# Two blocks on one core: the low weights' buffers and the low parts of the streamed operands at other places in a partition

## The chip, the cores and the metric

The kernel runs on one core of a Trainium2 chip. The metric is the device time of one execution in microseconds. TensorE multiplies, VectorE (DVE) and ScalarE (ACT) do elementwise work, GpSimd (POOL) helps, and SyncE (SP) issues most of the transfers. The operands lie in the core's on-chip memory, which has 128 partitions; an address below is a byte offset within a partition, and it is the same in all 128.

## The reference

Two blocks run one behind the other on 256 tokens of width 1024, all in float32. The first is one layer, the second adds 16 meta tokens (272 in all) and has two layers:

```python
# first block (first_block, hybrid_layer)
h = rmsnorm(x); proj = h @ w_in            # q, k, v, z, beta, decay, LRU input and gate
mix = concat(gated delta rule, gated linear recurrence)
x = x + mix @ w_out
u = relu(rmsnorm(x) @ w_ff1); x = x + (u * u) @ w_ff2      # d_ff 4096
# second block, twice
h = h + 0.5 * swiglu(rmsnorm(h))                           # d_ff 2816
h = h + mixer(rmsnorm(h))    # stick-breaking attention, a 31-tap convolution, two gates, w_out
h = h + 0.5 * swiglu(rmsnorm(h))
```

Each block ends in an RMS norm, and the meta tokens are dropped at the end. The second layer of the second block needs the meta tokens only for its first swiglu and for keys, values and the convolution, so part of its work runs on 256 tokens.

## The kernel before

**Products in two parts.** Nearly all time goes into products of a weight matrix with an activation of 256 or 272 columns. Both are split into a high part (rounded to float32r) and a low part (the rest). `job` (L508) makes one 128-row tile of a product: for each slice k of 128 rows it issues three matmuls into one PSUM bank, high weights times high activation (L534), high weights times low activation (L535) and low weights times high activation (L536). The weights are the stationary operand, 128 x 128, loaded anew for each matmul; the activation is streamed, 128 x 256 or 128 x 272.

**The weights.** `emit_dma` (L449) brings chunks of the packed weights into `raw` buffers. `emit_high` (L467) copies a unit of up to eight slices into one of five `wh` buffers on ScalarE. `emit_split` (L483) subtracts on VectorE (for some units on GpSimd) and writes one of four `wl` buffers. All `wh` and `wl` buffers are 4096 bytes, and slice s of a unit starts 512 s bytes into its buffer. The pools are opened in the order const, raw, wh, wl, small, tmp, and then the pool of each phase, and they lie in memory in that order.

**The streamed operands.** A class `XS` (L641) holds an activation as a high and a low tile, `hi(k)` and `lo(k)`. The narrow ones (8 slices) use one of two places in the const pool, `x0` and `x1`, each a pair of tiles (`x00`, `x01` and `x10`, `x11`) with a step of 320 elements (1280 bytes) at 272 columns and 256 elements at 256. Before each pair lies an unused tile `skew0` or `skew1` of `SKEW[i]` elements (L672). The wide ones, `hid` (32 slices in the first block, 22 in the swiglus), are two tiles of a pool of their own; the high one starts `pad` elements into its tile, with `pad` from `HSKEW`. Its keys are "ff1" for the first block and (first or second swiglu, layer) for the second. 

**Which stage reads what.** In the order of time: the projections of the first block read x0 (24 tiles), its w_out x1 (8), ff1 x0 (32) and ff2 `hid` "ff1" (8 tiles of 32 slices), all with 256 columns. Then, with 272 columns: layer 0's first gate/up (44 tiles) reads x1 and its down (8 tiles of 22 slices) `hid` (0,0); its mixer reads x0 (36 tiles), the attention's and the convolution's outputs in x1 and w_out's operand `mo` in x0; its second gate/up reads x1 and its down `hid` (1,0); layer 1's first gate/up reads x0, its down `hid` (0,1). Layer 1's mixer reads x1, partly with 272 columns and, for q and the gates, with 256 columns from token 16 on, which starts each slice 64 bytes later. Then 256 columns to the end: the attention's and convolution's outputs in x0, `mo` in x1, the last gate/up in x0 and the last down in `hid` (1,1).

**Order.** The order of the instructions on each engine is fixed when the program is written. A planner keeps an estimated clock for each engine (`clk`, advanced by `op` and by `job`) and interleaves the elementwise flows with the matmuls by it. Its costs depend on the engine, the kind of operation and the number of columns.

Of the kernel before, what the change touches and what calls it, by code (L numbers as in the profile page):

```python
# [7 lines left out]
F32 = mybir.dt.float32  # L8
F32R = mybir.dt.float32r
# [9 lines left out]
KD = 8  # L19
# [3 lines left out]
MIX1 = 17100  # L23
MIX2 = 16200
XW = 320
SKEW = (32, 32)
HSKEW = {"ff1": 56, (0, 0): 24, (0, 1): 8, (1, 0): 40, (1, 1): 40}
LEAD = 3
MINLEAD = 2
RAW = 3  # L30
# [195 lines left out]
def tile_hybrid_blocks(  # L226
# [13 lines left out]
    const = ctx.enter_context(tc.tile_pool(name="const", bufs=1))  # L240
    rawp = ctx.enter_context(tc.tile_pool(name="raw", bufs=RAW))
    whp = ctx.enter_context(tc.tile_pool(name="wh", bufs=LEAD + 2))
    wlp = ctx.enter_context(tc.tile_pool(name="wl", bufs=LEAD + 1))
    small = ctx.enter_context(tc.tile_pool(name="small", bufs=2))
    tmp = ctx.enter_context(tc.tile_pool(name="tmp", bufs=1))
# [90 lines left out]
    def start_flow(gen, rank=0, limit=None):  # L336

        f = Flow(gen)
        f.limit = limit
        f.t, f.eng, f.rank = main.t, "P", rank  # L340
        flows.append(f)
        flows.sort(key=lambda f: f.rank)
        return f
# [95 lines left out]
    def cv(name, i=None):  # L439
        o, w = CST[name]  # L440
        return C[:, o:o + w] if i is None else C[:, o + i:o + i + 1]
# [66 lines left out]
    def job(kind, x, n, o=0, bank_=None, last=True, start=None):  # L508


        j = job_no[0]
        job_no[0] += 1
        assert jobs[j][0] == kind, (jobs[j], kind)
        first = bank_ is None if start is None else start
        if bank_ is None:
            if len(free_banks) < 3:
                force(lambda: len(free_banks) >= 3)
            bank_ = free_banks.pop(0)
        acc = bank_[:, 0:n]
        mine = job_units[j]  # L520
        total = sum(len(units[u][1]) for u in mine)
        done = 0
        for u in mine:
            st["unit"] = u
            emit_split(u + MINLEAD)
            h, lo = wh.pop(u), wl.pop(u)
            clk["P"] = max(clk["P"], w_at.pop(u) + LAT)
            for i, k in enumerate(units[u][1]):
                if x.ev[k].t is None:
                    force(lambda: x.ev[k].t is not None)  # L530
                clk["P"] = max(clk["P"], x.ev[k].t + LAT)
                s = slice(128 * i, 128 * i + 128)
                xh, xl = x.hi(k, o, n), x.lo(k, o, n)
                nc.tensor.matmul(acc, h[:, s], xh, start=first and done == 0, stop=False)  # L534
                nc.tensor.matmul(acc, h[:, s], xl, start=False, stop=False)  # L535
                nc.tensor.matmul(acc, lo[:, s], xh, start=False, stop=last and done == total - 1)  # L536
                done += 1
                clk["P"] += 3 * n / 2400 + 0.007
                main.t, main.eng = clk["P"], "P"
                tick()  # L540
        return bank_
# [99 lines left out]
    class XS:  # L641

        def __init__(self, n, k=KD, pool=None, name=None, place=None, first=0, pad=0):
            w = -(-n // 64) * 64
            if pool is not None:
                self.place = None
                both = []
                for i in range(2):  # L650
                    t = pool.tile([128, k * w + pad * (i == 0)], F32R, name=f"{name}{i}")
                    both.append(t[:, pad * (i == 0):])
            else:
                self.place = place or places.pop(0)
                both = [p[:, first * w:(first + k) * w] for p in self.place]
            self.h, self.l = [a.rearrange("p (a b) -> p a b", a=k)[:, :, 0:n] for a in both]
            self.n = n
            self.ev = [Event() for _ in range(k)]
# [10 lines left out]

    places = []  # L670
    for i in range(2):
        const.tile([128, SKEW[i]], F32, name=f"skew{i}")  # L672
        places.append(tuple(const.tile([128, KD * XW], F32R, name=f"x{i}{j}") for j in range(2)))

    def X(k):
        return H[:, k, NM:T2]
# [50 lines left out]
    def first_norm():  # L727
        for k in range(KD):
            cur[0].t = 5.5 if k < 4 else 7.7
            now(split_scaled(X(k), cv("norm_mix_w", k), xa.hi(k), xa.lo(k)))  # L730
            note(xa.ev[k])
            if k < KD - 1:
                yield "W"
# [4 lines left out]
    f = start_flow(first_norm())  # L738
# [521 lines left out]
    for i, (c, t) in enumerate(ORDER1):  # L1260
        off = {"q": 0, "k": 4, "v": 8}.get(c, 0)
        b = job(c.upper(), xa, T1)
# [46 lines left out]
    for m in range(0, KD, 2):  # L1309
        if len(free_banks) < 3:  # L1310
            force(lambda: len(free_banks) >= 3)
        b = free_banks.pop(0)
# [4 lines left out]
    for m in range(0, KD, 2):  # L1317
        b = held[m // 2]
# [9 lines left out]
    phase = ExitStack()  # L1328
    hid = XS(T1, FF1, phase.enter_context(tc.tile_pool(name="ff1", bufs=1)), "hid", pad=HSKEW["ff1"])

# [84 lines left out]
    def swiglu(x, ev_r, o, n, next_g, old_phase, skew, final=False):  # L1415

        old_phase.close()
        phase = ExitStack()
        hid = XS(n, FF2, phase.enter_context(tc.tile_pool(name="ff2", bufs=1)), "hid", pad=HSKEW[skew])
        first = T2 - x.n  # L1420

        def half(ev):
            yield from wait(ev_r)
            ts(R5[:, 0:n], R[:, 0:n], 0.5, MUL)
            note(ev)

        def evac(ga, ua, m):
            yield from wait(ev_r)
            gs, hs_ = (yield from slot()), (yield from slot())
            g, h = gs[:, 0:n], hs_[:, 0:n]  # L1430
            tt(g, ga[:, 0:n], R[:, 0:n], MUL)
            give(ga)
            act(g, g, AF.Silu)
            yield "V"
            tt(h, g, ua[:, 0:n], MUL)
            give(ua)
            free_tmps.append(gs)
            yield from split(h, hid.hi(m), hid.lo(m))
            free_tmps.append(hs_)
            note(hid.ev[m])  # L1440

        ev5 = Event()
        start_flow(half(ev5))
        for m in range(FF2):
            if m == 0 and "gate" in PAIRED:
                ga, ua = pair(("gate", "up"), x, n, o - first)
            else:
                ga = job("gate", x, n, o - first)
                ua = job("up", x, n, o - first)
            start_flow(evac(ga, ua, m))  # L1450
        x.done()
        nx = None if final else XS(T2)
        ev_sq = Event()
        force(lambda: ev5.t is not None and (final or ev_h.t is not None))
        for m in range(KD):
            b = job("down", hid, n)
            if final and m == KD // 2:
                act(warm, ones[:, 0:1], AF.Sqrt)
            start_flow(
                residual(b, m, nx, None if final else next_g(m), acc1[:, 0:n], ev_sq, o, R5[:, 0:n])  # L1460
            )
        return nx, ev_sq, phase
# [281 lines left out]
    def norm_of(n, ev_sq):  # L1744
        ev = Event()
        start_flow(norm_rows(acc1[:, 0:n], n, 1.0 / 1024, 1e-6, R[:, 0:n], [ev_sq], ev, RC[:, 0:len(starts(n))]))
        return ev

    x, ph, ev_r = xc, ff1_phase, ev_r3
    for layer in range(2):  # L1750
        o = NM * layer
        n = T2 - o
        x, ev_sq, ph = swiglu(x, ev_r, 0, T2, lambda m: cv(f"mix_norm_2.{layer}", m), ph, (0, layer))
        x, ev_sq, ph = mixer(x, norm_of(T2, ev_sq), layer, lambda m: cv(f"ffn2_norm_2.{layer}", m), ph)
        x, ev_sq, ph = swiglu(x, norm_of(n, ev_sq), o, n, lambda m: cv("ffn1_norm_2.1", m), ph, (1, layer), final=layer == 1)
# [112 lines left out]
```

## Time and profile before

| | |
|---|---|
| runs | 1538.99, 1542.58, 1542.88 us, median 1542.58 |
| the profiled execution | 1540.48 us, its span 1538.8 |
| mean granted TensorE clock | 0.993 |
| TensorE, VectorE, ScalarE, GpSimd busy | 97%, 70%, 52%, 13% of the span |
| transfers | 248.58 MB, mean 162 GB/s |

The numbers behind the table come from one execution. A row of a timeline has the start in us, the duration, engine, line, operation, the tiles written and read, and the shapes. Matmuls overlap: the time from one start to the next is what one of them costs in a row of many.

### The profile page before, as it was taken

Reading aid. Unit: us, or ns where it says so; the run is one execution under the profiler, and the core shown is the slowest. Engines: PE = TensorE matmul, PEld = TensorE weight load, DVE = VectorE, ACT = ScalarE, POOL = GpSimd, SP = SyncE. Lnnn points to the kernel's source line nnn. Section 1 sums busy time; section 2 is a strip of 40 time slices with the busy share of each in tenths; the row PEclk is TensorE's granted clock in tenths of the full one; section 3 lists DMA queues with packets and bytes.
Section 4 is the critical chain, followed back from the end, with each engine's and each line's share of the span. In section 5 each row is a group of like instructions: output and inputs, shape, how many; then the busy total and the mean of one; then the engine's idle time right before and its main releaser. Section 6 shows DMA issues by size and latency. Waiting matters only on the chain.

```text
span 1538.8 us, 29451 instructions
## 1 busy us (share of the span) xinstructions
PE 1500.2 (97%) x12120; PEld 1480.3 (96%) x12120; DVE 1076.6 (70%) x1882; ACT 803.3 (52%) x1365; POOL 199.6 (13%) x236
## 2 busy tenths in 40 slices
PE   7999999999999999999999999999999999999997
PEld 6989999999999999998999999999999989999997
DVE  5887866667665668998766655655568996866654
ACT  4568666544544445555544444444444655654542
POOL 3230300000000022234400000000003234500000
PEclk9999999999999999999999999999999999999999
DMA  6312455554554444433555444545454433555552
GB/s 225 137 56 83 165 192 192 190 187 144 193 189 159 174 164 164 138 111 110 181 180 187 164 170 160 192 175 178 162 175 161 165 110 127 176 204 182 184 179 76
DMA packets 36376, 248.58 MB, mean 162 GB/s; under 512 B 3984, under 2 KB 5264, under 8 KB 12304
## 3 DMA queue, kind: packets, MB, share of 16 engines
q1 hardware_dynamic: 35248, 245.50, 45.5%
q8 instruction: 95, 1.56, 0.4%
q10 hardware_dynamic: 992, 1.19, 0.2%
q14 instruction: 41, 0.34, 0.1%
HBM read 245.63 MB, written 1.05 MB: 160 GB/s over the span
## 4 chain that ended last, share of the span: by engine, by line
PE 85%; DVE 10%; ACT 3%; issue 1%; POOL 1%; DMA 0%; DVEq 0%; SPq 0%; ACTq 0%; POOLq 0%
PE bank L535 27%; PE bank L536 27%; PE bank L534 27%; PE bank L319 4%; DVE arena L288 2%; DVE arena L299 2%; DVE wl L288 2%; DVE bank L299 1%; ACT arena L276 1%; PE bank L323 1%; DVE x L288 1%; DVE arena L315 1%; ACT wh L276 1%; POOL acc L311 0%; ACT x L276 0%
## 5 line engine op out<-in xcount | busy, mean ns | idle before, releaser
L534 PE MATMUL bank<-x,wh 128*128 128x272 f32 (+1 forms) x2752 | 797.9, 290 | 9.8 <-ACT x L276 9.2
L536 PE MATMUL bank<-x,wl 128*128 128x272 f32 (+1 forms) x2752 | 786.9, 286 | 5.5 <-DVE wl L288 4.7
L535 PE MATMUL bank<-x,wh 128*128 128x272 f32 (+1 forms) x2752 | 787.3, 286 | 2.9 <-DVE x L288 2.2
L288 DVE TENSOR_TENSOR wl<-raw,wh 128x1024 fp32r<-128x1024 f32 (+4 forms) x453 | 532.9, 1178 | 199.0 <-PE bank L536 175.6
L276 ACT ACTIVATE wh<-raw 128x1024 fp32r<-128x1024 f32 (+4 forms) x510 | 494.6, 976 | 271.2 <-PE bank L535 162.4
L534 PEld LDWEIGHTS bank<-x,wh 128*128 128x128 f32 x2752 | 521.5, 190 | 12.9 <-ACT x L276 10.1
L536 PEld LDWEIGHTS bank<-x,wl 128*128 128x128 f32 x2752 | 521.6, 190 | 6.6 <-DVE wl L288 5.7
L535 PEld LDWEIGHTS bank<-x,wh 128*128 128x128 f32 x2752 | 522.0, 190 | 6.2 <-DVE x L288 4.4
L535 PE MATMUL bank<-hid,wh 128*128 128x272 f32 (+1 forms) x960 | 274.5, 286 | 0.0
L536 PE MATMUL bank<-hid,wl 128*128 128x272 f32 (+1 forms) x960 | 274.5, 286 | 0.0
L534 PE MATMUL bank<-hid,wh 128*128 128x272 f32 (+1 forms) x960 | 274.5, 286 | 0.0
L536 PEld LDWEIGHTS bank<-hid,wl 128*128 128x128 f32 x960 | 181.7, 189 | 0.0
L535 PEld LDWEIGHTS bank<-hid,wh 128*128 128x128 f32 x960 | 180.6, 188 | 0.0
L534 PEld LDWEIGHTS bank<-hid,wh 128*128 128x128 f32 x960 | 180.6, 188 | 0.0
L493 POOL TENSOR_TENSOR wl<-raw,wh 128x512 fp32r<-128x512 f32 (+3 forms) x57 | 107.2, 1891 | 190.7 <-ACT wh L276 93.0
L288 DVE TENSOR_TENSOR tmp<-bank,R 128x272 f32<-128x272 f32 (+1 forms) x184 | 78.9, 430 | 68.1 <-PE bank L536 67.3
L276 ACT ACTIVATE tmp<-tmp 128x272 f32<-128x272 f32 (+1 forms) x140 | 59.3, 425 | 115.0 <-DVE tmp L288 78.7
L299 DVE SCALAR_TENSOR_TENSOR bank<-arena,C,bank 128x272 f32<-128x272 f32 (+1 forms) x232 | 102.4, 492 | 3.7 <-ACT bank L276 2.5
L1481 POOL MEMSET arena<- 64x1088 f32 (+1 forms) x4 | 3.9, 976 | 773.9 <-PE bank L536 773.9
L288 DVE TENSOR_TENSOR hid<-tmp,hid 128x272 fp32r<-128x272 f32 (+1 forms) x120 | 51.8, 433 | 38.0 <-ACT hid L276 38.0
L276 ACT ACTIVATE x<-H,C 128x272 fp32r<-128x272 f32 (+2 forms) x64 | 30.0, 486 | 83.5 <-DVE H L288 83.1
L276 ACT ACTIVATE hid<-tmp 128x272 fp32r<-128x272 f32 (+1 forms) x120 | 51.0, 426 | 42.3 <-DVE tmp L288 40.6
(200 smaller groups left out, 948.6 us busy)
## 6 DMA issues: line engine op xcount, KB each, us to landing
raw<-in_w_dram SPq DMA_DIRECT2D x187, 1024.0 KB, 4.8
raw<-in_w_dram SPq DMA_DIRECT2D x32, 960.0 KB, 4.7
raw<-in_w_dram SPq DMA_DIRECT2D x16, 896.0 KB, 4.6
raw<-in_w_dram SPq DMA_DIRECT2D x2, 512.0 KB, 5.9
H<-in_xt_dram SPq DMA_DIRECT2D x1, 544.0 KB, 6.5
LG<-in_lgw_dram SPq DMA_DIRECT2D x1, 512.0 KB, 6.0
out_dram<-H SPq DMA_DIRECT2D x2, 256.0 KB, 2.2
LM<-in_cm_dram SPq DMA_DIRECT2D x1, 320.0 KB, 5.2
```

The source lines that it names most:

```text
L276: nc.scalar.activation(out, in_, func, scale=scale, **kw)
L288: nc.vector.tensor_tensor(out=out, in0=a, in1=b, op=fn)
L299: nc.vector.scalar_tensor_tensor(out=out, in0=a, scalar=s, in1=b, op0=op0, op1=op1)
L315: nc.vector.tensor_tensor_scan(out=out, data0=a, data1=b, initial=initial, op0=op0, op1=op1)
L319: nc.tensor.matmul(out, lhsT, rhs, start=start, stop=stop)
L323: nc.tensor.transpose(out, in_, identity)
L493: nc.gpsimd.tensor_tensor(out=lo[:, 0:n], in0=raw[c][:, o:o + n], in1=wh[i][:, 0:n].bitcast(F32), op=SUB)
L534: nc.tensor.matmul(acc, h[:, s], xh, start=first and done == 0, stop=False)
L535: nc.tensor.matmul(acc, h[:, s], xl, start=False, stop=False)
L536: nc.tensor.matmul(acc, lo[:, s], xh, start=False, stop=last and done == total - 1)
L1481: nc.gpsimd.memset(QZ[i].f[64 * (1 - i):64 * (1 - i) + 64], 0.0)
```

## The change

The tile `gap` of 64 bytes stands in a pool between `wh` and `wl`, and nothing reads or writes it. The unused tiles `skew0` and `skew1` go; in their stead each tile of x0 and x1 has a lead of its own, and `hid`'s low tile has one too.

```diff
-SKEW = (32, 32)
-HSKEW = {"ff1": 56, (0, 0): 24, (0, 1): 8, (1, 0): 40, (1, 1): 40}
+SKEW = ((64, 16), (48, 0))
+HSKEW = {"ff1": (40, 16), (0, 0): (40, 32), (1, 0): (40, 48), (0, 1): (40, 16), (1, 1): (40, 0)}
...
     whp = ctx.enter_context(tc.tile_pool(name="wh", bufs=LEAD + 2))
+    skew = ctx.enter_context(tc.tile_pool(name="skew", bufs=1))
+    skew.tile([128, 16], F32, name="gap")
     wlp = ctx.enter_context(tc.tile_pool(name="wl", bufs=LEAD + 1))
...
-        def __init__(self, n, k=KD, pool=None, name=None, place=None, first=0, pad=0):
+        def __init__(self, n, k=KD, pool=None, name=None, place=None, first=0, pad=(0, 0)):
...
                 for i in range(2):
-                    t = pool.tile([128, k * w + pad * (i == 0)], F32R, name=f"{name}{i}")
-                    both.append(t[:, pad * (i == 0):])
+                    t = pool.tile([128, k * w + pad[i]], F32R, name=f"{name}{i}")
+                    both.append(t[:, pad[i]:])
...
     for i in range(2):
-        const.tile([128, SKEW[i]], F32, name=f"skew{i}")
-        places.append(tuple(const.tile([128, KD * XW], F32R, name=f"x{i}{j}") for j in range(2)))
+        both = [const.tile([128, SKEW[i][j] + KD * XW], F32R, name=f"x{i}{j}") for j in range(2)]
+        places.append(tuple(b[:, a:] for a, b in zip(SKEW[i], both)))
```

What this does to the addresses follows from the declared sizes, tile by tile in their order and each rounded up to 32 bytes. x0's pair starts at 36,096 and 46,336 before, at 36,224 and 46,528 after; x1's at 56,704 and 66,944, then 56,960 and 67,200; the first `wh` buffer at 104,640, then 104,896; the first `wl` buffer at 125,120, then 125,440; the phases' pools at 152,992, then 153,312. The table gives the start of each streamed operand, and of `wl`, less the start of `wh`, modulo 256 bytes. Slices (steps of 512, 1024 or 1280 bytes) and buffers (4096) do not change these numbers.

| operand | before: hi, lo | after: hi, lo | after: lo less `wl` |
|---|---|---|---|
| `wl` | 0 | 64 | |
| x0 | 64, 64 | 192, 0 | 192 |
| x1 | 192, 192 | 192, 192 | 128 |
| x1 read from token 16 on | 0, 0 | 0, 0 | 192 |
| `hid` "ff1" | 192, 192 | 192, 0 | 192 |
| `hid` (0,0) | 64, 64 | 192, 64 | 0 |
| `hid` (1,0) | 128, 128 | 192, 128 | 64 |
| `hid` (0,1) | 0, 0 | 192, 0 | 192 |
| `hid` (1,1) | 128, 128 | 192, 192 | 128 |

## The prediction

> **What bounds the kernel now.** First the page: the busy line and the chain that ended last.
>
> ```profile
> span 1538.8 us, 29451 instructions
> ...
> PE 1500.2 (97%) x12120; PEld 1480.3 (96%) x12120; DVE 1076.6 (70%) x1882; ACT 803.3 (52%) x1365; POOL 199.6 (13%) x236
> ...
> PE 85%; DVE 10%; ACT 3%; issue 1%; POOL 1%; DMA 0%; DVEq 0%; SPq 0%; ACTq 0%; POOLq 0%
> PE bank L535 27%; PE bank L536 27%; PE bank L534 27%; PE bank L319 4%; DVE arena L288 2%; DVE arena L299 2%; DVE wl L288 2%; DVE bank L299 1%; ACT arena L276 1%; PE bank L323 1%; DVE x L288 1%; DVE arena L315 1%; ACT wh L276 1%; POOL acc L3
> ```
>
> The end is set by the three matmuls of `job`, 81% of the span. What counts is therefore the time from one of their starts to the next; their durations (near 0.29 us) overlap. I read it from the timeline of TensorE: first and last row of a stretch without a gap, divided by the steps between. With 272 columns:
>
> ```profile
> 399.82 0.28 PE L534 MATMUL bank<-x,wh 128*128 128x272 f32 x1
> ...
> 407.34 0.29 PE L535 MATMUL bank<-x,wh 128*128 128x272 f32 x1
> ...
> 899.73 0.29 PE L535 MATMUL bank<-hid,wh 128*128 128x272 f32 x1
> ...
> 907.58 0.29 PE L534 MATMUL bank<-hid,wh 128*128 128x272 f32 x1
> ...
> 999.77 0.29 PE L535 MATMUL bank<-x,wh 128*128 128x272 f32 x1
> ...
> 1007.50 0.29 PE L536 MATMUL bank<-x,wl 128*128 128x272 f32 x1
> ...
> 1099.71 0.29 PE L535 MATMUL bank<-hid,wh 128*128 128x272 f32 x1
> ...
> 1107.57 0.29 PE L534 MATMUL bank<-hid,wh 128*128 128x272 f32 x1
> ```
>
> With "gap" as in the table of the change (start of a streamed operand less start of `wh`, modulo 256 bytes): layer 0's first gate/up stage reads x1 (gap 192): 7.52 us over 61 steps, 123.3 ns. Layer 1's reads x0 (gap 64), same code, same shape: 7.73/61 = 126.7 ns. The `hid` products at gap 128 (899.73) and at gap 0 (1099.71): 7.85/62 = 126.6 and 7.86/62 = 126.8. So one residue of four is 3.4 ns a matmul quicker, and 256 bytes is a usable period: slices step by 1280 bytes for x and 512 for weights, and the pace does not alternate with them. With 256 columns:
>
> ```profile
> 299.73 0.28 PE L535 MATMUL bank<-hid,wh 128*128 128x256 f32 x1
> ...
> 306.91 0.28 PE L536 MATMUL bank<-hid,wl 128*128 128x256 f32 x1
> ...
> 1279.82 0.28 PE L535 MATMUL bank<-x,wh 128*128 128x256 f32 x1
> ...
> 1283.90 0.28 PE L536 MATMUL bank<-x,wl 128*128 128x256 f32 x1
> ...
> 1329.80 0.28 PE L536 MATMUL bank<-x,wl 128*128 128x256 f32 x1
> ...
> 1336.94 0.28 PE L536 MATMUL bank<-x,wl 128*128 128x256 f32 x1
> ...
> 1399.79 0.28 PE L534 MATMUL bank<-x,wh 128*128 128x256 f32 x1
> ...
> 1406.97 0.28 PE L535 MATMUL bank<-x,wh 128*128 128x256 f32 x1
> ```
>
> ff2 on `hid` (gap 192): 7.18/61 = 117.7 ns. Layer 1's gates on x1, read 16 tokens on (gap 0): 4.08/34 = 120.0. Its o2 on x1 (gap 192): 7.14/63 = 113.3. Its last gate/up on x0 (gap 64): 7.18/61 = 117.7. So at 256 columns gap 192 occurs with two paces, 113.3 and 117.7, and the gap alone does not settle it.
>
> **What the change adds and removes.** No instruction, transfer, semaphore or wait is added, removed or moved: `gap` is never read or written, and `op` counts columns, not addresses, so the planner emits the same order and no queue is passed. Only the pace can change. Which pair of addresses matters is not shown, because before, hi, lo, `wh` and `wl` of a stage always shared one gap. The one hint is when the next weights are read:
>
> ```profile
> 399.82 0.19 PEld L535 LDWEIGHTS bank<-x,wh 128*128 128x128 f32 x1
> ```
>
> The load for the second matmul (L535) starts with the first matmul (L534, 399.82 above). I take the likeliest reading: **a stream meets the weights loaded beside it.** Then L534 and L536 (hi, with `wh` loading) depend on hi less `wh`: 192 everywhere after the change, but 0 for x1 read 16 tokens on. L535 (lo, with `wl` loading) depends on lo less `wl`: 192 for x0, ff1 and (0,1), 128 for x1 and (1,1), 0 for (0,0), 64 for (1,0). At 192 I use 123.3, elsewhere 126.7. That the *place* 128 itself is quick, whatever the weights are, would give hi the same, x1 no loss and x0's lo no gain: -8.2 in place of the -8.1 us below before the mixer's half is taken off, so both share the sum.
>
> - x0, 272 columns, layer 1's first gate/up: 22 x 2 x 8 x 3 = 1056 matmuls, all three at 192: 1056 x 3.33 ns = -3.5 us.
> - x0, layer 0's mixer: 864 (36 tiles) and its o2 192, again 1056: -3.5 us, counted at half:
>
> ```profile
> 559.00:697.00 138.00, 135.85 (x1033) 131.20 (x1033) 122.25 (x248) 73.12 (x157) 43.31 (x70) 1.00 0.37 131
> ```
>
>   This row of the stages' view has VectorE at 122.25 of 138 us, so a quicker TensorE soon waits for it: -1.8 us (ends 0 and -3.5).
> - `hid`, 8 x 22 x 3 = 528 each: (0,1) all three, -1.8; (0,0) and (1,0) two of three, 704 x 3.33 = -2.3.
> - x1, 272 columns: 1056 + 192 + 1056 + 384 = 2688 matmuls; the 896 L535 leave 192 for 128: 896 x 3.33 = +3.0.
> - 256 columns: x0 (192, 1056 and 1344 in the first block) and ff1's hid (768) move to or stay at 192 in every pair. From 117.7 they could go to 113.3 or, by the 120.0 row, up. I take 117.7, as ff2's row is at 192 too and is the longest such stretch (268 to 358 us): 0, ends -4.4 and +2.3 ns each. x1's o2 (192) may lose 113.3 in one of three or wholly: +0.3 to +0.8; (1,1) and the gates read 16 tokens on may gain as much. Together 0.
>
> Sum: -3.5 - 1.8 - 1.8 - 2.3 + 3.0 = -6.4 us.
>
> What hides the supply at the quicker pace: the row of the groups for layer 1's gate/up stage, 954 to 1089 us.
>
> ```profile
> L288 DVE TENSOR_TENSOR wl<-raw,wh 128x1024 fp32r<-128x1024 f32 x43 | 52.5, 1223 | 28.6 <-PE bank L536 26.8 <-ACT hid L276 1.3 <-ACT wh L276 0.4
> ```
>
> VectorE idles 26.8 us there until TensorE frees a `wl` buffer; 3.5 us less leaves it cover. It also covers writes to the new places: 43 subtractions could each take 0.5 us longer before TensorE saw it. Should they, that stage loses its gain first.
>
> The Trainium skill, "SBUF — State Buffer", section "Who interferes with whom", speaks against all this: TensorE has two independent read ports, one for the moving operand and one for weights, and never waits on anyone. By it the pace would not depend on places and the sum would be 0. The two gate/up rows (123.3 and 126.7 ns) disagree, since shape and code are equal and the places differ; it stays a rival.
>
> **The rivals.**
> 1. **The weights already in the array count**, not those being loaded: L534 hi less `wh` 192; L535 lo less `wh`: 192 for x1 only; L536 hi less `wl`: 128 everywhere. Then x0 gains in one of three (704 matmuls, a half hidden: -1.7), `hid` in one (-1.8), x1 loses in one (+3.0), o2 loses its 113.3 (+0.8): +0.3, 1540.8 us. Against it: the load rows start with the matmul before.
> 2. **Slower: the quick pace needs all three alike.** Place: x1 at 272 columns, now at 123.3. Its lo is off by 64 from where it stood against `wl`. If one odd pair in three drops the whole triple to 126.7, 2688 x 3.33 = +9.0; o2 falls from 113.3 to 117.7, 192 x 4.4 = +0.8, and nothing else gains: +9.8, 1550.3 us. It decides once an odd L535 delays the next load too. For it: 113.3 against 117.7 at one gap shows that the pace is a pattern the stream falls into, not a sum of three prices. Against it: nothing before had mixed gaps.
> 3. **The pace does not hang on places.** The quick and slow stretches then differ by something else in their stages: 1540.5 us. Against it: the two gate/up stages are equal in all but data and place. This is the case of the Trainium skill's rule above.
> 4. **`gap` takes no room** because nothing uses it; `wl` stays with `wh` and `hid` starts 64 bytes lower (hi gap 128, no gain). Then x0 gains in two of three, 1408 x 3.33 less a quarter = -3.5: 1537.0 us. Against it: x0 and x1 lie 20,480 bytes plus the unused tile `skew1` apart, which is a multiple of 256 without it, and still have different paces.
> 5. **256 columns fall into 113.3:** 768 (ff1) + 768 (ff2) + 192 + 1056 = 2784 matmuls x 4.4 = -12.2 on top: 1521.9 us.
>
> **How the numbers follow.** The profiled execution took 1540.48 us: span 1538.8 and 1.7 around it; the median of the runs is 1542.58, 2.1 above, within their spread of 1538.99 to 1542.88. 1540.5 - 6.4 = **1534 us**. Chances: forecast 0.45, rival 1 0.20, rival 2 0.15, rival 3 0.08, rival 4 0.05, rival 5 0.07. The range takes in rival 2 up to 1550 and three quarters of the way from the forecast to rival 5: **1525 to 1550**; alone the forecast has 1530 to 1538 (mixer hidden wholly or not at all, 256 columns by about 1 ns). A measurement tells 0.3% (4.6 us) from no change. Forecast and rival 5 are mostly faster by more, 0.48; rivals 1, 3 and 4 and the forecast's upper end are within, 0.36; rival 2 is slower, 0.16.
>
> **What would show it.** In the timeline of after: x0's and (0,1)'s 272-column stretches at 123.3; (0,0), (1,0) and x1 at (2 x 123.3 + 126.7)/3 = 124.4. x1 at 126.7 is rival 2; x0 still at 126.7 with x1 between is rival 1; every stretch as before is rival 3; `hid` unmoved and x1 at 123.3 is rival 4; 113.3 in ff1 and the last gate/up is rival 5. Wrong altogether would be a pace beyond 113.3 to 126.7, which mixed gaps may bring and no row of before can exclude.

## The result

The changed kernel takes 1552.8 us (median of 4 runs, 1552.06 to 1552.89) against 1541.53 for the kernel before (4 runs, 1538.99 to 1542.88): ratio 1.0074, 95% interval 1.006 to 1.0087. It is slower by 0.74%, 11.3 us, where 6.4 us less were forecast. The page of its profiled execution begins so:

```profile
span 1551.1 us, 29451 instructions
## 1 busy us (share of the span) xinstructions
PE 1509.9 (97%) x12120; PEld 1489.8 (96%) x12120; DVE 1076.2 (69%) x1882; ACT 803.8 (52%) x1365; POOL 197.6 (13%) x236
```

The instructions are the same, and of the busy times only TensorE's has grown by more than 1 us (1500.2 to 1509.9; its weight loads, PEld, with it). In the changed file the three matmuls of `job` are L536, L537 and L538. The timeline of TensorE, read as before (first and last row of a stretch over the steps between); columns are start, duration, engine, line, tiles, shapes:

```profile
399.83 0.29 PE L537 MATMUL bank<-x,wh 128*128 128x272 f32 x1
...
407.31 0.29 PE L536 MATMUL bank<-x,wh 128*128 128x272 f32 x1
...
519.81 0.29 PE L536 MATMUL bank<-hid,wh 128*128 128x272 f32 x1
...
527.52 0.29 PE L538 MATMUL bank<-hid,wl 128*128 128x272 f32 x1
...
999.71 0.29 PE L536 MATMUL bank<-x,wh 128*128 128x272 f32 x1
...
1007.50 0.29 PE L538 MATMUL bank<-x,wl 128*128 128x272 f32 x1
...
1339.74 0.28 PE L536 MATMUL bank<-x,wh 128*128 128x256 f32 x1
...
1346.95 0.28 PE L537 MATMUL bank<-x,wh 128*128 128x256 f32 x1
```

The time between two starts, the pace, follows. x1 at 272 columns: 7.48 us over 59 steps, 126.8 ns (123.3 before). `hid` (0,0): 7.71/62 = 124.4 (126.7). x0: 7.79/62 = 125.6 (126.7). x1's o2 at 256 columns: 7.21/61 = 118.2 (113.3). By stages, each from its first matmul of `job` to that of the next, the twelve microseconds lie here:

| stage | before us | after us | difference | pace before, after (ns) |
|---|---|---|---|---|
| first block: projections, x0 | 133.5 | 135.3 | +1.8 | 117.8, 118.5 |
| its w_out, x1 | 33.5 | 33.7 | +0.2 | 113.3 and 117.8, 118.3 |
| ff1, x0 | 93.7 | 95.6 | +1.9 | 117.8, 118.5 |
| ff2, `hid` "ff1" | 90.5 | 91.0 | +0.5 | 117.8, 118.5 |
| layer 0 gate/up 1, x1 | 133.6 | 137.0 | +3.4 | 123.3, 126.7 |
| down 1, `hid` (0,0) | 66.9 | 65.8 | -1.1 | 126.7, 124.4 |
| mixer with o2, x0, x1, x0 | 196.0 | 194.9 | -1.1 | x0 126.7, 125.6 and 122.2 |
| gate/up 2, x1 | 132.3 | 135.7 | +3.4 | 123.3, 126.7 |
| down 2, `hid` (1,0) | 66.8 | 66.3 | -0.5 | 126.7, 125.6 |
| layer 1 gate/up 1, x0 | 135.4 | 134.2 | -1.2 | 126.7, 125.6 |
| down 1, `hid` (0,1) | 66.9 | 66.3 | -0.6 | 126.7, 125.6 |
| mixer with o2, x1, x0, x1 | 183.6 | 188.3 | +4.7 | o2 113.3, 118.2 |
| gate/up 2, x0 | 125.7 | 126.5 | +0.8 | 117.8, 118.5 |
| down 2, `hid` (1,1) | 62.5 | 62.3 | -0.2 | 118.7, 118.2 |

Together +12.0 of the 12.3 us between the spans. Three of the rows hold more than pace. In the projections pace gives 0.4 us (576 x 0.7 ns); the rest is the granted clock, whose means over 7 to 20, 20 to 40, 40 to 60 and 60 to 80 us are 0.89, 0.81, 1.00 and 0.91 after and 0.92, 0.97, 0.91 and 0.91 before, 1.8 us of work less after, which covers it. ff1's matmuls are 0.7 ns slower, 0.6 us in 768; for the rest there is the granted clock again, which stood at 0.86 for 12 us (12 x 0.14 = 1.7 us of work). In the stages' view PEclk is the third number from the end; first after, then before:

```profile
180.00:192.00 12.00, 10.03 (x73) 9.83 (x72) 9.62 (x23) 7.43 (x15) 3.10 (x3) 0.86 0.61 201
```

```profile
180.00:192.00 12.00, 9.98 (x85) 9.99 (x86) 10.09 (x24) 7.40 (x15) 1.99 (x3) 1.00 0.61 218
```

And layer 1's o2, 26.0 us before and 30.2 after, lost only 192 x 4.9 ns = 0.9 us to its pace. The other 3.3 us are a wait of TensorE for VectorE's last write of `x`. First after, then before (in brackets the idle time before an instruction and what ended it):

```profile
1328.85 2.38 POOL L495 TENSOR_TENSOR wl<-raw,wh 128x1024 fp32r<-128x1024 f32 x1 [2.76 <-ACT wh L278]
1328.95 2.57 DVE L290 TENSOR_TENSOR x<-arena,x 128x256 fp32r<-128x256 f32 x1
1331.57 0.58 PE L537 MATMUL bank<-x,wh 128*128 128x256 f32 x1 [3.61 <-DVE x L290]
```

```profile
1321.95 0.42 DVE L288 TENSOR_TENSOR x<-arena,x 128x256 fp32r<-128x256 f32 x1
1322.25 2.40 POOL L493 TENSOR_TENSOR wl<-raw,wh 128x1024 fp32r<-128x1024 f32 x1 [3.16 <-PE bank L536]
```

In all eleven profiles of this document the length of that write goes with the order of these two starts: where GpSimd's subtraction starts first, by 0.04 to 0.10 us, the write takes 2.57 to 2.60 us (seven profiles); where VectorE starts first, by 0.05 to 0.31 us, it takes 0.42 (four). The places do not set that order: the three profiles of one kernel, everything at 192 below, stand on both sides.

By this, about 6 of the twelve microseconds (an estimate: 1.4 in the projections, 1.3 in ff1 and 3.3 in o2) are clock and this wait, and about 6 are pace.

The pace itself is not one number for x0 in layer 0's mixer, though its places do not change there (192, 0 and `wl` at 64). The first two rows are one stretch, the last two a later one, after a pause at 616 us:

```profile
580.58 0.29 PE L536 MATMUL bank<-x,wh 128*128 128x272 f32 x1
...
591.88 0.29 PE L536 MATMUL bank<-x,wh 128*128 128x272 f32 x1
...
617.85 0.28 PE L536 MATMUL bank<-x,wh 128*128 128x272 f32 x1
...
631.04 0.28 PE L536 MATMUL bank<-x,wh 128*128 128x272 f32 x1
```

11.30 us over 90 steps are 125.6 ns, 13.19 over 108 are 122.1, below the quickest pace that 272 columns had before. The granted clock is 1.00 in both.

### The profile page after: what moved, and what is told of

Its sections match the earlier page's. It is cut to its first block, busy times and chain, and to the rows that moved or that the text cites. A ratio compares the mean times of both kernels' runs of the same rounds, so it can differ in the third digit from the quotient of the medians.

```text
span 1551.1 us, 29451 instructions
## 1 busy us (share of the span) xinstructions
PE 1509.9 (97%) x12120; PEld 1489.8 (96%) x12120; DVE 1076.2 (69%) x1882; ACT 803.8 (52%) x1365; POOL 197.6 (13%) x236
## 5 line engine op out<-in xcount | busy, mean ns | idle before, releaser
L536 PE MATMUL bank<-x,wh 128*128 128x272 f32 (+1 forms) x2752 | 800.2, 291 | 9.5 <-ACT x L278 8.8
L537 PE MATMUL bank<-x,wh 128*128 128x272 f32 (+1 forms) x2752 | 792.5, 288 | 6.5 <-DVE x L290 5.8
L538 PE MATMUL bank<-x,wl 128*128 128x272 f32 (+1 forms) x2752 | 793.8, 288 | 4.9 <-DVE wl L290 4.2
L290 DVE TENSOR_TENSOR wl<-raw,wh 128x1024 fp32r<-128x1024 f32 (+4 forms) x453 | 531.0, 1174 | 204.3 <-PE bank L538 170.3
L536 PEld LDWEIGHTS bank<-x,wh 128*128 128x128 f32 x2752 | 524.4, 191 | 12.6 <-ACT x L278 9.6
L537 PEld LDWEIGHTS bank<-x,wh 128*128 128x128 f32 x2752 | 524.9, 191 | 9.9 <-DVE x L290 8.1
L538 PEld LDWEIGHTS bank<-x,wl 128*128 128x128 f32 x2752 | 522.4, 190 | 6.2 <-DVE wl L290 5.1
L537 PE MATMUL bank<-hid,wh 128*128 128x272 f32 (+1 forms) x960 | 273.6, 285 | 0.0
L536 PE MATMUL bank<-hid,wh 128*128 128x272 f32 (+1 forms) x960 | 273.6, 285 | 0.0
L538 PE MATMUL bank<-hid,wl 128*128 128x272 f32 (+1 forms) x960 | 273.5, 285 | 0.0
L537 PEld LDWEIGHTS bank<-hid,wh 128*128 128x128 f32 x960 | 181.6, 189 | 0.0
L536 PEld LDWEIGHTS bank<-hid,wh 128*128 128x128 f32 x960 | 181.1, 189 | 0.0
L538 PEld LDWEIGHTS bank<-hid,wl 128*128 128x128 f32 x960 | 180.4, 188 | 0.0
L495 POOL TENSOR_TENSOR wl<-raw,wh 128x512 fp32r<-128x512 f32 (+3 forms) x57 | 105.8, 1867 | 192.9 <-ACT wh L278 95.1
L290 DVE TENSOR_TENSOR tmp<-bank,R 128x272 f32<-128x272 f32 (+1 forms) x184 | 78.9, 430 | 66.9 <-PE bank L538 66.1
```

The source lines that it names most:

```text
L290: nc.vector.tensor_tensor(out=out, in0=a, in1=b, op=fn)
L495: nc.gpsimd.tensor_tensor(out=lo[:, 0:n], in0=raw[c][:, o:o + n], in1=wh[i][:, 0:n].bitcast(F32), op=SUB)
```

## The experiments

Three numbers in brackets are the places hi, lo and `wl` less `wh`, modulo 256. The forecast's theory: a stream meets the weights that are loaded beside it, so only hi less `wh` and lo less `wl` count, each matmul by itself. The main rival: the quick pace needs all three alike.

### One part alone: the streams' new places

The gap tile goes behind the `wl` pool, so that only `wl` returns.

```diff
-    skew = ctx.enter_context(tc.tile_pool(name="skew", bufs=1))
-    skew.tile([128, 16], F32, name="gap")
     wlp = ctx.enter_context(tc.tile_pool(name="wl", bufs=LEAD + 1))
+    skew = ctx.enter_context(tc.tile_pool(name="skew", bufs=1))
+    skew.tile([128, 16], F32, name="gap")
```

> The 64-byte tile stands behind the wl buffers instead of ahead of them, so wl is back at gap 0 and every other address is that of the changed kernel. Forecast theory (a stream meets the weights loaded beside it): x1 at 272 columns back to 123.3 ns; x0 (192, 0) and the three hid stages keep 192 in two pairs of three and have lo less wl at 0, 64, 128 and 0, so 124.4 each; about 8 us under the kernel before. Rival (the quick pace needs hi, lo and wl alike): x1 123.3, x0 and hid 126.7, the kernel before's time within 1 us at 272 columns. If wl's place has nothing to do with the loss, x1 stays at 126.7.

Measured: 1536.83 us against 1541.15, ratio 0.9976 (0.9962 to 0.9991). Its timeline:

```profile
399.83 0.28 PE L538 MATMUL bank<-x,wl 128*128 128x272 f32 x1
...
407.36 0.29 PE L536 MATMUL bank<-x,wh 128*128 128x272 f32 x1
...
999.76 0.29 PE L537 MATMUL bank<-x,wh 128*128 128x272 f32 x1
...
1007.60 0.29 PE L537 MATMUL bank<-x,wh 128*128 128x272 f32 x1
```

x1: 7.53/61 = 123.4. x0: 7.84/63 = 124.4; the three `hid` stages have 124.4 to 124.5 too, whether lo stands at 0, 64 or 128. As a mean that is the forecast's price to the decimal: two matmuls of three at 123.3, one at 126.7. The single steps are not so: in layer 1's first gate/up, from L536, L537 and L538 to the next start, they have means of 123.4, 125.0 and 125.0 ns. The rival's 126.7 is out. But only 4.3 of the expected 8 us arrived. The 272-column stages gave theirs (135.4 to 133.0 us in layer 1's first gate/up); the first block's projections and ff1 were slower in this profile than before, 135.0 against 132.1 and 95.1 against 93.6 from first to last matmul, at the old pace of 117.8 in most of ff1. The granted clock was lower there: 0.80, 1.00 and 0.83 over 20 to 40, 40 to 60 and 60 to 80 us against 0.97, 0.91 and 0.91, and 0.89 against 1.00 over 176 to 192 us. That is one profile each; what the other executions lost there is not known.

### The other part alone: `wl` 64 bytes on

```diff
-SKEW = ((64, 16), (48, 0))
-HSKEW = {"ff1": (40, 16), (0, 0): (40, 32), (1, 0): (40, 48), (0, 1): (40, 16), (1, 1): (40, 0)}
+SKEW = ((32, 0), (32, 0))
+HSKEW = {"ff1": (40, 0), (0, 0): (8, 0), (1, 0): (24, 0), (0, 1): (56, 0), (1, 1): (24, 0)}
```

> Only wl moves by 64; hi and lo stand as before the change in every stage (x0 64, x1 192, hid 192, 64, 128, 0, 128). Forecast theory: lo less wl is 0 for x0, 128 for x1, 192 for hid (0,1); so x0 126.7, x1 124.4, hid (0,1) 125.6. Rival (all three alike): 126.7 everywhere at 272 columns, since x1 loses its pace and nobody gains, +9 to +10 us on the kernel before. The changed kernel had x1 at these very gaps at 126.7, so the same again would lay its loss to wl alone.

Measured: 1548.74 us (one execution; 1541.15 for the kernel before on the same chip).

```profile
399.76 0.29 PE L536 MATMUL bank<-x,wh 128*128 128x272 f32 x1
...
407.37 0.29 PE L536 MATMUL bank<-x,wh 128*128 128x272 f32 x1
```

x1: 7.61/60 = 126.8, as in the changed kernel, and not the forecast theory's 124.4. `hid` stays at 126.7 for (128, 128, 64) and (0, 0, 64), but x0 and `hid` (0,0), now (64, 64, 64), gain: 125.6. So the rival, which had 126.7 everywhere, misses as well. The loss of x1 belongs to `wl`'s 64 bytes alone.

### The same within one stage

All streams at 192 (the edit of the next section) and every second unit's low weights 64 bytes into their buffers:

```diff
-            lo = wlp.tile([128, 1024], F32R, tag="wl", name="wl")
+            lo = wlp.tile([128, 1088], F32R, tag="wl", name="wl")
+            lo = lo[:, 16 * (i % 2):]
```

> All streams at 192, and every second unit's low weights 64 bytes into their buffer, so that units with wl at 0 and at 64 follow each other in every stage. If wl's place beside the streams is what cost x1 its pace, units of 272 columns go in turn at 123.3 and 126.7 (mean 125.0) in every such stage, x0 and hid included. If it was something that holds for a whole stage (another load on the memory, what the stage before left behind), one pace for all units of a stage.

Measured: 1541.95 us (one execution). Three units of 24 matmuls begin in layer 1's first gate/up with these rows of the timeline; the middle one has `wl` at 0:

```profile
996.27 0.28 PE L535 MATMUL bank<-x,wh 128*128 128x272 f32 x1
...
999.31 0.29 PE L535 MATMUL bank<-x,wh 128*128 128x272 f32 x1
...
1002.27 0.28 PE L535 MATMUL bank<-x,wh 128*128 128x272 f32 x1
```

3.04/24 = 126.7 ns, then 2.96/24 = 123.3. Over all 272-column units, the steps from one slice to the next inside a unit and without a pause have means of 123.4 ns a matmul at `wl` 0 (873 of them) and 126.5 at 64 (905). The units follow each other in one stage, so a load elsewhere or the stage's history is excluded: the place of the low weights sets the pace, unit by unit. VectorE's writes of later `wl` buffers alternate with the units too, but one such write takes 1.22 us of a unit's 3.0 (the mean in layer 1's first gate/up), and at 64 the steps from the second to the seventh of a unit all have means between 126.58 and 126.66 ns. The Trainium skill's rule, named in the prediction ("SBUF — State Buffer", "Who interferes with whom"), has TensorE's two read ports independent and TensorE waiting on no one. By the prediction's reading of it the pace would not depend on places, and these rows disagree; which of the two reads loses the time they do not show.

### Everything at 192

```diff
-SKEW = ((64, 16), (48, 0))
-HSKEW = {"ff1": (40, 16), (0, 0): (40, 32), (1, 0): (40, 48), (0, 1): (40, 16), (1, 1): (40, 0)}
+SKEW = ((0, 0), (0, 0))
+HSKEW = {"ff1": (56, 0), (0, 0): (56, 0), (1, 0): (120, 0), (0, 1): (56, 0), (1, 1): (120, 0)}
...
-    skew = ctx.enter_context(tc.tile_pool(name="skew", bufs=1))
-    skew.tile([128, 16], F32, name="gap")
```

> No gap tile, no leads for x0 and x1, and leads for hid such that hi and lo stand at 192 against both wh and wl in every stage, except in x1 read from token 16 on (0). Both theories: 123.3 ns in every 272-column stage, 2112 + 1584 matmuls x 3.33 = 12.3 us less than before, 8 to 11 after what VectorE hides in the mixer. At 256 columns the residue modulo 512 tells what chooses between 113.3 and 117.7: x0 and the last hid stand at 192 of 512 as x1 did in the 113.3 stretch, hid of the first block at 448 as it did at 117.7. If 512 decides, x0 goes to 113.3 and takes off another 8 to 9 us in its 2016 steady matmuls; if not, 117.7 and no more.

Measured: 1525.53 us against 1541.15, ratio 0.9911 (0.9884 to 0.9938), single runs from 1522.21 to 1533.68. In the profile, 1533.68 us:

```profile
999.81 0.29 PE L536 MATMUL bank<-x,wl 128*128 128x272 f32 x1
...
1007.58 0.28 PE L536 MATMUL bank<-x,wl 128*128 128x272 f32 x1
...
1399.81 0.28 PE L534 MATMUL bank<-x,wh 128*128 128x256 f32 x1
...
1406.99 0.28 PE L535 MATMUL bank<-x,wh 128*128 128x256 f32 x1
```

x0 at 272 columns: 7.77/63 = 123.3, and so in every 272-column stage. The last gate/up at 256: 7.18/61 = 117.7. So 512 does not decide between 113.3 and 117.7. The spread of the runs suggested a pattern that each execution falls into. Two more profiles of the same kernel:

> The kernel with everything at 192, profiled a second time. Its times spread from 1522.2 to 1533.7 us, and its profiled execution, 1533.7, had 117.8 ns in ff1, ff2, the last gate/up and the last down. If the pace of the 256-column stages at (192, 192, 0) is a pattern that each execution falls into, one or more of these four stages goes at 113.3 in a quicker execution, each worth 2.3 to 4.7 us, and the 272-column stages stay at 123.3. If the spread comes from elsewhere, the four stay at 117.8.

> The same again: another draw of the 256-column stages if they are a matter of each execution, the same stages at the same paces as in the first profile if not.

Measured: 1526.23 and 1527.49 us. The second, at the same place:

```profile
1399.78 0.28 PE L535 MATMUL bank<-x,wh 128*128 128x256 f32 x1
...
1406.92 0.28 PE L535 MATMUL bank<-x,wh 128*128 128x256 f32 x1
```

7.14/63 = 113.3, in the last gate/up and the last down of both; they took 121.1 and 59.7 us instead of 125.5 and 62.1. ff1 and ff2 stayed at 117.8 in all three. One program, one set of addresses, two paces. These two profiles are from another chip, where the kernel before took 1549.78 us in its one run, but a single execution shows the same. In the first profile the projections, all from x0's same places, hold these two stretches (two rows each) with a pause between:

```profile
34.21 0.28 PE L534 MATMUL bank<-x,wh 128*128 128x256 f32 x1
...
40.33 0.28 PE L534 MATMUL bank<-x,wh 128*128 128x256 f32 x1
...
42.96 0.28 PE L534 MATMUL bank<-x,wh 128*128 128x256 f32 x1
...
49.32 0.28 PE L534 MATMUL bank<-x,wh 128*128 128x256 f32 x1
```

6.12 us over 54 steps are 113.3 ns, 6.36 over 54 are 117.8, with the granted clock at 1.00 in both. So at these places the pace is a pattern that the stream fell into anew after a pause; what chooses it was not found.

### `wl` at 128 and 192

The gap tile is made 32, then 48 elements long; hi stands at 192 everywhere, lo at all four places.

```diff
-    skew.tile([128, 16], F32, name="gap")
+    skew.tile([128, 32], F32, name="gap")
...
+SKEW = ((0, 48), (16, 0))
+HSKEW = {"ff1": (24, 0), (0, 0): (24, 16), (1, 0): (24, 32), (0, 1): (24, 0), (1, 1): (24, 32)}
```

> wl 128 from wh; hi at 192 everywhere; lo at 192 (x1, ff1, hid (0,1)), 128 (x0), 0 (hid (0,0)) and 64 (hid (1,0), (1,1)). Forecast theory: lo less wl is 64, 0, 128 and 192 in that order, so 124.4 for all at 272 columns but 123.3 for hid (1,0). Rival (all three alike): 126.7 everywhere. A pace under 123.3 anywhere would be new to both.

> wl 192 from wh, hi at 192, lo at 192 (x1, ff1, hid (0,1)), 128 (x0), 0 (hid (0,0), (1,1)) and 64 (hid (1,0)): the row that the table of paces by lo and wl still lacks. The forecast's rule (only lo less wl counts, one of three) would give lo less wl 0, 192, 64 and 128, so 123.3 for x0 and 124.4 for the others at 272 columns. It already missed at wl 64 and 128 whenever lo less wl was 192, so x0 at 124.4 or above is what I expect; nothing under 123.3.

For 192 the leads of `hid` are 8 and 0, 16, 32, 0, 16. Measured: 1547.53 and 1557.31 us (one execution each). With the runs above, the paces at 272 columns and hi at 192 are, in ns:

| lo | `wl` 0 | `wl` 64 | `wl` 128 | `wl` 192 |
|---|---|---|---|---|
| 192 | 123.3 | 126.7 | 124.5 | 125.6 |
| 128 | 124.5 | 125.6 | 126.7 | 124.9 and 131.1 |
| 64 | 124.5 | 124.5 | 124.5 | 125.5 |
| 0 | 124.5 | 125.6 and 122.2 | 124.4 | 125.5 |

The forecast's rule makes a diagonal quick, lo less `wl` 192: the cells (192, 0), (0, 64), (64, 128), (128, 192). Only the first is. "All alike" has one quick cell and 126.7 elsewhere; the other fifteen hold six paces. A sum of a part for lo and a part for `wl` doesn't fit either: going from `wl` 0 to 64 costs 3.4 at lo 192, 1.1 at 0 and nothing at 64. Two cells have both of their values: at (192, 128, 192) x0 went at 124.9 in layer 1's first gate/up and at 131.1 in layer 0's o2, and at (192, 0, 64) at 125.6 and 122.2 in the changed kernel, as shown above. (192, 128, 128) has the value of that gate/up and went at 124.4 in part of the mixer. So the table has what most matmuls did, not what a place must give. What came unexpected is ff2, at (192, 192, 128) in the run with `wl` at 128:

```profile
299.80 0.28 PE L538 MATMUL bank<-hid,wl 128*128 128x256 f32 x1
...
306.94 0.28 PE L538 MATMUL bank<-hid,wl 128*128 128x256 f32 x1
```

7.14/63 = 113.3 ns through the whole stage, 87.0 us against 90.3 before.

### `wl` by the width of the product

Everything at 192, `wl` at 0 for units of 272 columns and at 128 for units of 256 (but for layer 1's q and gates, whose `wl` stays at 0):

```diff
+    def narrow(j):
+        kind, name, layer = j[:3]
+        if not name.endswith("_2"):
+            return 1
+        return int(layer == 1 and (kind in ("ys", "yc", "o2") or name.startswith("ffn2")))
...
-            lo = wlp.tile([128, 1024], F32R, tag="wl", name="wl")
+            lo = wlp.tile([128, 1088], F32R, tag="wl", name="wl")
+            lo = lo[:, 32 * narrow(jobs[units[i][0]]):]
```

> All streams at 192 as in the run with everything at 192, and wl by the width of the product: gap 0 for units of 272 columns, 128 for units of 256 columns (the wl buffers are 4352 bytes, and the low parts of those units start 128 bytes into them). If a stage's pace hangs on the three places alone, as the run with wl at 128 showed 113.3 ns for hid of the first block at (192, 192, 128): ff1, ff2, the last gate/up and the last down at 113.3 instead of 117.8, 272 columns at 123.3; 3120 steady matmuls x 4.4 = 13.8 us under the run with everything at 192, so some 1511 to 1514 us. If the 113.3 of that stage was a pattern it fell into by chance, 117.8 again in some of the four and about 1520 to 1526.

Measured: 1520.01 us against 1540.41, ratio 0.987 (0.9848 to 0.9892), single runs from 1518.48 to 1523.27. It is quicker than both kernels.

```profile
span 1518.3 us, 29451 instructions
```

```profile
1399.83 0.28 PE L542 MATMUL bank<-x,wh 128*128 128x256 f32 x1
...
1406.97 0.28 PE L542 MATMUL bank<-x,wh 128*128 128x256 f32 x1
```

The last gate/up: 7.14/63 = 113.3, and the projections, ff1, ff2, the last down and o2 as well; the 272-column stages keep 123.3. Against the first profile of everything at 192 the span is 13.7 us shorter, 13.0 of it in ff1, ff2, the last gate/up and the last down, where 13.8 were expected. The expected time, 1511 to 1514 us, was missed all the same: it took the 13.8 off the median of that kernel, and the medians lie only 5.5 us apart. Two of that kernel's three profiles had 113.3 in the last gate/up and down already. At (192, 192, 128) no 256-column stage settled at 117.8, in this kernel or in the one with `wl` at 128 throughout.

## Why the prediction was wrong, step by step

- **What bounds the kernel**: right. The order of instructions and VectorE's work did not move (1076.6 and 1076.2 us busy), and the difference is the matmuls' pace, with the granted clock and one wait for VectorE in layer 1's o2.
- **"At 192 I use 123.3, elsewhere 126.7", each matmul by itself and lo against the `wl` loaded beside it**: this is the step that failed. With `wl` at 0 it gives the right means (124.4 for every other lo); of the twelve cells with `wl` elsewhere nine differ from it, and none of the three on its diagonal is at 123.3 (125.6 and 122.2, 124.5, 124.9 and 131.1). Which pair of reads meets when is not settled; the runs exclude the three rules that were stated and leave a table. In every run the first `wh` buffer starts at 192 modulo 256, so they do not tell places measured from `wh` from places in the partition either.
- **One pace for one place**: the prediction read it off single stretches. The profile of before has two paces already in x1's own stage at 192, layer 0's first gate/up, where this stretch stands between two pauses:

```profile
366.28 0.29 PE L534 MATMUL bank<-x,wh 128*128 128x272 f32 x1
...
371.60 0.29 PE L534 MATMUL bank<-x,wh 128*128 128x272 f32 x1
```

  5.32 us over 42 steps are 126.7 ns, with the granted clock at 1.00. It is short, and 123.3 holds for nearly all of the rest.
- **x1, +3.0**: the largest miss. Not a third but the whole triple fell to 126.7: 2688 x 3.4 = 9.1 us by pace, of which 6.8 show in its two gate/up stages and the rest lies in mixers that other work fills. `wl` alone does it.
- **x0, -3.5 and -1.8**: 125.6 in place of 123.3, and 122.2 in one stretch of the mixer; -1.2 and -1.1.
- **`hid`, -1.8 and -2.3**: (0,1) -0.6, (0,0) and (1,0) -1.6. (0,0) at 124.4 was as forecast, by a cell in which the rule happens to hold.
- **256 columns, 0**: 2400 x 0.7 = 1.7 us by pace in x0's three long stages (4.5 in the table, with the clock), 0.5 in ff2, 0.9 in o2. The bounds given, 113.3 and 120.0, held.
- **Cover of the supply, no cost of the new places for VectorE**: right; its subtraction into `wl` took 1174 ns on the mean, 1178 before.
- **Rivals.** The slower one named x1 and 126.7, with 1550.3 us, and is right in place (x1 at 126.7) and near in size, the size in part by luck, since about 6 of the twelve us are not pace. Its mechanism, all or nothing, is out: x0 and `hid` gained, and x1 with `wl` at 128 goes at 124.5. Rival 1 had x1 at 124.4 and falls. Rival 3 falls with the alternating units, rival 4 with `hid` (0,0) at 124.4. Rival 5's pace exists at 192 with `wl` at 128, and in some stretches with `wl` at 0, but no 256-column stage of the changed kernel settled at it.
- **The chance of a slower time, 0.16**, was too small for what the section itself said last, that no row of before could price mixed places. In each stage of before hi, lo, and the weights among themselves stood alike; a rule with three free places had been read off one line of them.

## What to carry to other kernels

Where TensorE is the bound and its weights are reloaded for each matmul, read the time between starts by stage; if equal shapes have unequal paces, compare the operands' addresses modulo a few hundred bytes before anything else. Measure a small table of places (streams and weights each moved alone) rather than reason from pairs, read several stretches for each place, since the pace can change after a pause, and move one operand at a time: here the streams alone gained 0.24%, `wl` alone cost 0.5% in its one run, and the two chosen together gave -1.3%. Before a difference of a few microseconds is put down to the change, look for a single long wait and for the granted clock in the same stage. A place that works for one width need not work for another.

## What the runs showed of the hardware that was not expected

- A matmul of 272 columns goes at 122.2 to 131.1 ns and one of 256 columns at 113.3 to 122.2 (ff2 at (192, 192, 192)) with the same instructions and other starts of three operands, in steps of 64 bytes. In the alternating units the place of one operand alone makes it 123.4 or 126.5. The Trainium skill, "TensorE: Matmul & The Clock Gate", section "Back-to-back issue gap", gives N/2.4 + 2.5 ns for a matmul by itself, without time for weight loads, 115.8 and 109.2 here by estimate; no run reached them.
- The pace is not a function of the places alone. At (192, 192, 0) and 256 columns two stretches of one execution went at 113.3 and 117.8, and the last gate/up at 117.7 in one execution and at 113.3 in two others; at (192, 0, 64) and 272 columns two stretches of one execution went at 125.6 and 122.1.
- A VectorE write of 128 x 256 elements took 0.42 us when it started ahead of a GpSimd subtraction and 2.57 to 2.60 when it started up to 0.10 us behind one.
